# An encoder block on one core: all attention ahead of the MLP, and the MLP as two seven-product passes

## The chip, the core and the metric

The kernel runs on one core of one Trainium2 chip. The core has a matmul engine (TensorE, PE, with its weight loads shown as PEld), VectorE (DVE), ScalarE (ACT), GpSimd (POOL), and SyncE (SP), which here only issues DMAs. The metric is device time in microseconds (us). The kernel before takes 2292.17 us (median of 3 runs, 2291.84 to 2292.46).

## The reference

One layer of a hybrid encoder on 2048 tokens of width 1024, with 16 meta tokens ahead. All arithmetic is to fp32 accuracy.

```python
hn = rms_norm(h, g_mix); proj = hn @ w_in          # 1024 x 1536
q, k, v, u = ...                                   # 4 query heads, 2 key heads of 128; u: 4 groups of 128
q, k = axial_rope(rms_norm(q, g_q)), axial_rope(rms_norm(k, g_k))
attn = softmax(q @ k.T / sqrt(128)) @ v            # all 2064 keys
four = fft2(u).real @ w_fourier                    # per group
h = h + concat(rms_norm(attn), rms_norm(four)) @ w_out
m = rms_norm(h, g_mlp)
h = h + square(relu(m @ w_up)) @ w_down            # 1024 x 4096, 4096 x 1024
return rms_norm(h, g_final)[:, 16:]
```

## The kernel before

**Products.** Most products are split: each fp32 operand becomes hi + lo in a faster format (fp32r), by a cast on ACT and a subtraction on DVE (`split`, L70 and L71, or L73 and L74 with a scale), and `mm3` (L80 to L82) makes three matmuls, hi x hi, hi x lo, lo x hi. A plain fp32 product is one call without splits.

**Attention.** The generator `attention()` works in 16 units: a unit is 256 tokens and one key head with its two query heads, 512 columns. For each of 16 tiles of 128 keys and a last one of 96 rows (`REM`, the meta keys), `scores` makes three matmuls into s, ACT copies s to S, and DVE takes running maxima M of pairs. At the end of a unit `stats` turns M into mb (transposes on PE, a maximum on DVE, transposes, a copy on ACT). `softmax` subtracts mb on DVE, takes exponents on ACT, sums into acc on DVE, and multiplies with v on PE into o. Where a unit is below `NATIVE` (2 here, units 0 and 1), the value product is plain fp32 (L842, o<-S,vn); else the exponent is split (ph on ACT, pl on DVE) and `mm3` is used. While unit u is in `softmax`, unit u+1 is in `scores`, LAG tiles behind. `finish` divides by the row sums and stores o_d. A unit is 20 steps of the generator.

**What stands beside it.** `Att.upto(n)` runs the generator up to step n, and `mix(gen, n, a0, a1)` spreads steps a0 to a1 over the yields of another generator, so attention is laid between other work: the Fourier part (`four`) up to step `FLEAD` = 30, the Fourier half of the out-projection (`out_f`, 32 groups pof of 12 matmuls) up to the end of block 0, then the MLP of blocks 0 and 1 (`head`). A block is 512 tokens (`BLOCKS`). The tile framework orders the instructions of each engine once more when the program is built; the order is fixed from then on.

**The MLP.** The attention half of the out-projection of a block is `out_a` (poa, 96 matmuls), after which h is complete and its norm known. Blocks 0 and 1 go through `transposes`, `up` (pup, 8 groups of 192 matmuls) and `down` (pdn, the same), weights loaded and split once for each block. Blocks 2 and 3 go through one pass of 1024 tokens, in which 2 x 2 blocks of a matrix product are made of seven products instead of eight (`ORDER` = "1265734", with sums and differences of blocks on DVE): `flip_early` and `flip` scale and transpose h (block 2 through m_d in DRAM, by m and mt on ACT), `b_form` makes the seven moving operands BF, `up_weights` loads w_up in pieces R0 and R1 and forms seven stationary operands wuh, wul for each of 8 groups; the up products are ux and uy, stored to s_d in the forms that the down products need; the down products dx and dy are added to h (hs). The final norm and the stores to out follow each tile (`follow`, `store`). The last products of block 1's MLP (`up(1, 7)`, `down(1, 7)`) stand around `out_a(3)`, `flip(3)` and the forming of BF.

PSUM: `bank` takes one of 4 tiles, s and o and the transposes have others, and in the pass `ybank` has 4.

SP issues most DMAs in one order, POOL those of q, k and v.

Of the kernel before, what the change touches and what calls it, by code (L numbers as in the profile page):

```python
# [19 lines left out]
P = 128  # L20
# [20 lines left out]
NATIVE = 2  # L41
# [4 lines left out]
LEAD = 4  # L46
AHEAD = 30
FLEAD = 30
SKIP = 5
T_BUFS = (5, 6)  # L50
F_BUFS = (6, 7)
S_BUFS = 8
A_BUFS = 11
# [82 lines left out]
def encoder_block(ctx: ExitStack, tc: tile.TileContext, x, meta, w_in, w_f,  # L136
# [64 lines left out]
    m_d = dram.tile([P, KT, 512], F32, name="m_d")  # L201
# [530 lines left out]
    ended = []  # L732

    def attention():
# [70 lines left out]
        def softmax(u, i):  # L805
# [4 lines left out]
            if i == NT:  # L810
# [10 lines left out]
                ended[:] = [ins_of(nc.tensor.matmul(s["O"], vt[4][:MR], hi[:MR], start=False, stop=True))]  # L821
# [29 lines left out]
        def finish(u):  # L851
# [16 lines left out]
            if first:  # L868
                sqs[b] = ap2.tile([P, 256], F32, name=f"sq_{b}", tag="sq", bufs=3)
# [28 lines left out]

    HELD = 5
# [9 lines left out]
    def out_f():  # L909
# [103 lines left out]
    hp0 = Lines(tc.alloc_tile_pool(name="hp0", bufs=1, reuse_waits="tile"), small)  # L1013
    op_ = Lines(tc.alloc_tile_pool(name="op", bufs=1, reuse_waits="tile"), small)
    of = out_f()
    mix(itertools.islice(of, 34 - HELD), 34 - HELD, FLEAD, need[0])
    mix(of, HELD, need[0], need[0] + LEAD)
# [3 lines left out]

    hps = hp0, Lines(tc.alloc_tile_pool(name="hp1", bufs=1, reuse_waits="tile"), small)
    atp = Lines(tc.alloc_tile_pool(name="atp", bufs=1, reuse_waits="tile"), small)
    mp = Lines(tc.alloc_tile_pool(name="mp", bufs=1, reuse_waits="tile"), small)
    H, MT = {}, {}
# [4 lines left out]
    SC = {}  # L1030

    def out_a(b, beside=iter(())):
# [15 lines left out]
        sums = [mp.tile([P, 2], F32, name=f"hss_{b}_{t}", tag="hss", bufs=8) for t in range(T)]  # L1048
        A = (atp if b > 1 else ey).tile([P, 2, NQ, 512], R32, name=f"at_{b}", tag="at" if b > 1 else "e0")
# [4 lines left out]
        part = []  # L1054
        for half in range(2):
            c = slice(half * 512, (half + 1) * 512)
            pss = [bank(f"poa_{b}_{half}_{t}") for t in range(T)]
            ops = {}

            def products(t, k):  # L1060
                ts = slice(t * P, (t + 1) * P)
                a, w = ops[k]
                mm3(nc, pss[t], (a[0][:, ts], a[1][:, ts]), w, k == 0, k == NQ - 1)

            for k in range(NQ):
                w = wtile(w_out[k * P:(k + 1) * P, c], f"oa_{b}_{half}_{k}", c_ao(k))
                ops[k] = (A[:, 0, k], A[:, 1, k]), w
                if k < NQ - 2:
                    for t in range(T):
                        products(t, k)  # L1070
                    if half:
                        next(beside, None)
                    yield
            for t in range(T):
                for k in (NQ - 2, NQ - 1):
                    products(t, k)
                if t % 2:
# [12 lines left out]
        for t in range(T):  # L1090
            nc.vector.scalar_tensor_tensor(part[t], sums[t][:, 1:2], 1.0 / D, part[t], op0=ALU.mult, op1=ALU.add)
            if b < 2:
                nc.vector.reciprocal(SC[b][:, t:t + 1], part[t])
                continue
            tag = "rs_m2" if b == 2 else "rs_m"
            ms.append(mp.tile([P, 1], F32, name=f"{tag}_{b}_{t}", tag=tag, bufs=4))
            nc.gpsimd.tensor_tensor(ms[t], part[t], mhalf[:, :1], op=ALU.pow)
            nc.sync.dma_start(h_d[2 * b0 + t], hs[t])
        att.cap = need[b + 1] + AHEAD if b < 3 else 1 << 30

    def transposes(b):

        T = 2 * BLOCKS[b][1]
        mhl = [(ey if b or e == "l" else atp).tile([P, KT, 512], R32, name=f"mT{e}_{b}", tag=tag)
               for e, tag in zip("hl", ("e0" if b else "at", "e1"))]
        MT[b] = [(mhl[0][:, k, :T * P], mhl[1][:, k, :T * P]) for k in range(KT)]
        for kk in range(KT // 2):
            for k in (2 * kk, 2 * kk + 1):
                ps = app.tile([P, 512], F32, name=f"pmt_{b}_{k}", tag="S", bufs=2)
                for t in range(T):  # L1110
                    nc.tensor.transpose(ps[:, t * P:(t + 1) * P], H[b][t][:, k * P:(k + 1) * P], ident)
                split(mhl[0][:, k, :T * P], mhl[1][:, k, :T * P], ps[:, :T * P], c_mlp(k))
            yield

    def flip_early(b):

        hs, ms = H.pop(b), MT[b, "s"]
        for kk in range(KT // 2):
# [3 lines left out]
            for i in range(2):  # L1122
                k = 2 * kk + i
                ps = app.tile([P, 512], F32, name=f"pmt_{b}_{k}", tag="S", bufs=2)
# [4 lines left out]
                nc.sync.dma_start(m_d[:, k], raw)  # L1129
            yield  # L1130

    def up(b, grp):
        N = 256 * BLOCKS[b][1]
        f0 = grp * 512
        pss = [bank(f"pup_{b}_{grp}_{f}") for f in range(4)]
        ws = []
        for k in range(KT):
            w = wtile(w_up[k * P:(k + 1) * P, f0:f0 + 512], f"up_{b}_{grp}_{k}")
            ws.append(w)
            if k < KT - 2:  # L1140
                for f in range(4):
                    fs = slice(f * P, (f + 1) * P)
                    mm3(nc, pss[f][:, :N], (w[0][:, fs], w[1][:, fs]), MT[b][k], k == 0, False)
                yield
        for f in range(4):
            fs = slice(f * P, (f + 1) * P)
            for k in (KT - 2, KT - 1):
                mm3(nc, pss[f][:, :N], (ws[k][0][:, fs], ws[k][1][:, fs]), MT[b][k], False, k == KT - 1)
            if f % 2:
                yield  # L1150
        acts = []
        for f in range(4):
            r = a_tile(f"r_{b}_{grp}_{f}")[:, :N]
            nc.scalar.activation(r, pss[f][:, :N], AF.Relu)  # L1154
            nc.scalar.square(r, r)
            hl = tuple(a_tile(f"a{e}_{b}_{grp}_{f}", R32)[:, :N] for e in "hl")
            split(*hl, r)
            acts.append(hl)
        MT[b, grp] = acts

    def down(b, grp, halves=(0, 1)):
        T = 2 * BLOCKS[b][1]
        f0 = grp * 512
# [4 lines left out]
        if last:  # L1168
            sums = MT[b, "f"]
# [618 lines left out]
```

## Time and profile before

| | |
|---|---|
| median of 3 runs | 2292.17 us (2291.84 to 2292.46) |
| profiled execution: span | 2291.4 us |
| the same execution's granted TensorE clock, mean | 0.999 |
| PE busy | 2278.1 us, 10846 matmuls |
| DVE busy | 1718.7 us |
| ACT busy | 1280.6 us |
| DMA moved | 307.23 MB, mean 134 GB/s |
| first matmul of the seven-product pass | at 1674.2 us |

The profile shows one execution. Its span runs from the first to the last instruction. A row of a group of instructions has line, engine, operation, output and inputs, shapes and count, then busy time in us and the mean of one in ns, then the idle time before them and what ended it. Matmuls are pipelined: one is shown with 390 ns though the next starts some 227 ns later, so the busy time of PE hides short gaps, and its pace (matmuls per us) tells more.

### The profile page before, as it was taken

Reading aid. Unit: us, or ns where it says so; the run is one execution under the profiler, and the core shown is the slowest. Engines: PE = TensorE matmul, PEld = TensorE weight load, DVE = VectorE, ACT = ScalarE, POOL = GpSimd, SP = SyncE. Lnnn points to the kernel's source line nnn. Section 1 sums busy time; section 2 is a strip of 40 time slices with the busy share of each in tenths; the row PEclk is TensorE's granted clock in tenths of the full one; section 3 lists DMA queues with packets and bytes.
Section 4 is the critical chain, followed back from the end, with each engine's and each line's share of the span. In section 5 each row is a group of like instructions: output and inputs, shape, how many; then the busy total and the mean of one; then the engine's idle time right before and its main releaser. Section 6 shows DMA issues by size and latency. Waiting matters only on the chain.

```text
span 2291.4 us, 30005 instructions
## 1 busy us (share of the span) xinstructions
PE 2278.1 (99%) x10846; PEld 1883.0 (82%) x10846; DVE 1718.7 (75%) x2448; ACT 1280.6 (56%) x2303; POOL 184.0 (8%) x235
## 2 busy tenths in 40 slices
PE   9999999999999999999999999999999999999998
PEld 7888988777888888888888888888888888888887
DVE  6435588999986877986887877885875656697796
ACT  6443356566665655665765775664665545543344
POOL 2212120222000000000000100000000000200000
PEclk9999999999999999999999999999999999999999
DMA  6343252543533222333342453224454444865442
GB/s 213 100 119 102 78 169 79 190 137 120 166 117 108 96 87 79 114 114 106 97 157 87 157 175 104 92 82 170 140 177 158 152 152 156 303 193 165 129 138 83
DMA packets 178069, 307.23 MB, mean 134 GB/s; under 512 B 14960, under 2 KB 63728, under 8 KB 177536
## 3 DMA queue, kind: packets, MB, share of 16 engines
q1 hardware_dynamic: 159136, 262.89, 34.9%
q0 software_dynamic: 18640, 42.16, 6.2%
q8 instruction: 85, 1.39, 0.3%
q14 instruction: 64, 0.52, 0.1%
q10 hardware_dynamic: 144, 0.26, 0.0%
HBM read 225.27 MB, written 79.99 MB: 133 GB/s over the span
## 4 chain that ended last, share of the span: by engine, by line
PE 94%; DVE 3%; DMA 1%; ACT 1%; issue 1%; POOL 0%; SPq 0%; POOLq 0%; DVEq 0%; ACTq 0%
PE pdn L80 5%; PE pdn L82 5%; PE pdn L81 5%; PE pup L80 5%; PE pup L82 5%; PE pup L81 5%; PE s L80 3%; PE s L82 3%; PE s L81 3%; PE ux L80 2%; PE ux L81 2%; PE ux L82 2%; PE dx L80 2%; PE dx L82 2%; PE dx L81 2%; PE o L81 2%
## 5 line engine op out<-in xcount | busy, mean ns | idle before, releaser
L80 PE MATMUL pdn<-wh_dn,ah 128*128 128x512 f32 x512 | 201.5, 394 | 0.2 <-ACT r L1154 0.2
L80 PE MATMUL pup<-mTh,wh_up 128*128 128x512 f32 x512 | 201.5, 394 | 0.0
L81 PE MATMUL pup<-mTl,wh_up 128*128 128x512 f32 x512 | 200.7, 392 | 0.0
L82 PE MATMUL pup<-mTh,wl_up 128*128 128x512 f32 x512 | 200.4, 391 | 0.0
L81 PE MATMUL pdn<-wl_dn,ah 128*128 128x512 f32 x512 | 199.9, 390 | 0.0
L82 PE MATMUL pdn<-wh_dn,al 128*128 128x512 f32 x512 | 198.7, 391 | 0.0
L773 ACT COPY S<-s 128x512 f32<-128x512 f32 x256 | 148.4, 584 | 55.6 <-PE s L82 48.5
L70 ACT CAST wh_up<-wr_up 128x512 fp32r<-128x512 f32 x128 | 79.4, 620 | 164.3 <-PE pup L81 76.5
L832 DVE TENSOR_TENSOR S<-S,mb 128x1024 f32<-128x1024 f32 x128 | 154.8, 1218 | 8.4 <-ACT mb L803 8.2
L71 DVE TENSOR_TENSOR pl<-S,ph 128x512 fp32r<-128x512 f32 x196 | 132.3, 696 | 11.0 <-ACT ph L70 10.7
L833 ACT ACTIVATE S<-S 128x1024 f32<-128x1024 f32 x114 | 120.7, 1060 | 34.7 <-DVE S L832 34.1
L70 ACT CAST wh_dn<-wr_dn 128x512 fp32r<-128x512 f32 x128 | 79.1, 620 | 107.9 <-PE pdn L82 52.6
L71 DVE TENSOR_TENSOR wl_up<-wr_up,wh_up 128x512 fp32r<-128x512 f32 x128 | 87.6, 687 | 68.1 <-ACT wh_up L70 63.3
L839 DVE TENSOR_TENSOR acc<-acc,S 128x1024 f32<-128x1024 f32 x110 | 134.1, 1219 | 1.3 <-ACT S L833 1.1
L71 DVE TENSOR_TENSOR wl_dn<-wr_dn,wh_dn 128x512 fp32r<-128x512 f32 x128 | 87.2, 687 | 60.2 <-ACT wh_dn L70 51.8
L70 ACT CAST ph<-S 128x512 fp32r<-128x512 f32 x196 | 118.7, 620 | 15.9 <-PE o L82 12.5
L70 ACT CAST ah<-a 128x1024 fp32r<-128x1024 f32 x56 | 58.5, 1048 | 118.2 <-issue 60.8
L779 DVE TENSOR_TENSOR M<-M,S 128x1024 f32<-128x1024 f32 x96 | 118.0, 1229 | 6.7 <-ACT S L773 6.0
L80 PEld LDWEIGHTS pdn<-wh_dn,ah 128*128 128x128 f32 x512 | 96.1, 188 | 23.5 <-ACT r L1154 3.6
L80 PE MATMUL s<-q,kt 128*128 128x512 f32 (+1 forms) x272 | 113.0, 415 | 0.1
L82 PEld LDWEIGHTS pdn<-wh_dn,al 128*128 128x128 f32 x512 | 96.2, 188 | 19.9
L82 PEld LDWEIGHTS pup<-mTh,wl_up 128*128 128x128 f32 x512 | 96.2, 188 | 19.4
(345 smaller groups left out, 6413.0 us busy)
## 6 DMA issues: line engine op xcount, KB each, us to landing
wr_up<-in_w_up_dram SPq DMA_DIRECT2D x128, 256.0 KB, 2.8
wr_dn<-in_w_down_dram SPq DMA_DIRECT2D x128, 256.0 KB, 2.6
a<-s_d SPq DMA_DIRECT2D x42, 512.0 KB, 3.6
R<-in_w_up_dram SPq DMA_DIRECT2D x16, 1024.0 KB, 5.2
s_d<-s SPq DMA_DIRECT2D x64, 256.0 KB, 2.2
d<-in_w_down_dram SPq DMA_DIRECT2D x26, 512.0 KB, 5.0
s_d<-c SPq DMA_DIRECT2D x48, 256.0 KB, 2.4
x<-in_x_dram SPq DMA_DIRECT2D x16, 512.0 KB, 4.9
```

The lines of the kernel that those rows point to most:

```text
L70: self.high = nc.scalar.copy(hi, src)
L71: self.low = nc.vector.tensor_tensor(lo, src, f32v(hi), op=ALU.subtract)
L80: nc.tensor.matmul(out, a[0], b[0], start=first, stop=False, skip_group_check=chain)
L81: nc.tensor.matmul(out, a[0], b[1], start=False, stop=False, skip_group_check=chain)
L82: nc.tensor.matmul(out, a[1], b[0], start=False, stop=last, skip_group_check=chain)
L773: nc.scalar.copy(S[:, i % 2], ps)
L779: nc.vector.tensor_tensor(M, M, S, op=ALU.max)
L832: nc.vector.tensor_tensor(S, S, mb, op=ALU.subtract)
L833: nc.scalar.activation(p, S, AF.Exp, scale=ISQ)
L839: nc.vector.tensor_tensor(acc, acc, p, op=ALU.add)
```

## The change

- All 16 units make their value products in plain fp32 (`NATIVE` = 16), so v is loaded unsplit and p is not split.
- `up`, `down`, `transposes`, `flip_early`, `final` and `head` are gone. `out_a` keeps all of w_out's attention half in SBUF as splits (WO), goes tile by tile, and every block is turned by `flip` into m_d.
- Attention is laid beside the Fourier part up to step 84 (`FLEAD`), beside `out_f` up to step 210 (`OLEAD`), then 31 steps beside `out_a` and `flip` of block 0 and as many beside those of block 1; what is left is issued at the first yield of `out_a(2)`. `out_a(3)` and `flip(3)` come after attention.
- Then `up_pass` and `down_pass` run twice, for blocks 0 and 1 (pass 0) and 2 and 3 (pass 1). Beside pass 0's up products, `forms_ahead` makes the moving operands of pass 1 and stores them to f_d; pass 1 loads them.

```diff
-NATIVE = 2
+NATIVE = 16
-LEAD = 4
-AHEAD = 30
-FLEAD = 30
+FLEAD = 84
+OLEAD = 210
+STEPS_A = 31
-A_BUFS = 11
+A_BUFS = 6
...
-    m_d = dram.tile([P, KT, 512], F32, name="m_d")
+    m_d = [dram.tile([P, KT, 512], F32, name=f"m_d{b}") for b in range(4)]
+    f_d = {n: dram.tile([P, 2, 4, 512], F32, name=f"f_d{n}") for n in ORDER}
...
-    mix(itertools.islice(of, 34 - HELD), 34 - HELD, FLEAD, need[0])
-    mix(of, HELD, need[0], need[0] + LEAD)
+    mix(out_f(), 34, FLEAD, OLEAD)
...
+        MS[b] = ms = []
+        for t in range(T):
+            ts = slice(t * P, (t + 1) * P)
+            sums = mp.tile([P, 2], F32, name=f"hss_{b}_{t}", tag="hss", bufs=8)
+            for half in range(2):
+                c = slice(half * 512, (half + 1) * 512)
+                ps = bank(f"poa_{b}_{half}_{t}")
+                for k in range(NQ):
+                    mm3(nc, ps, (A[:, 0, k, ts], A[:, 1, k, ts]), WO[k, half], k == 0, k == NQ - 1)
+                nc.vector.scalar_tensor_tensor(hs[t][:, c], ps, ra[:, t:t + 1], hs[t][:, c], op0=ALU.mult, op1=ALU.add)
+                nc.scalar.activation(a_tile(f"hj_{b}_{t}_{half}"), hs[t][:, c], AF.Square,
+                                     accum_out=sums[:, half:half + 1])
+                yield
...
+    for b in range(3):
+        a0 = OLEAD + b * STEPS_A
+        mix(itertools.chain(out_a(b), flip(b)), 12 if b < 2 else 9, a0, a0 + STEPS_A if b < 2 else 1 << 20)
...
+    def forms_ahead(lf):
+
+        for k, i in itertools.product(range(4), range(2)):
+            r, c = {}, slice(i * 256, i * 256 + 256)
+            for n, b, kk in (("11", 2, k), ("21", 2, k + 4), ("12", 3, k), ("22", 3, k + 4)):
+                r[n] = lf.tile([P, 256], F32, name=f"lr{n}_{k}_{i}", tag="lr" + n)
+                nc.sync.dma_start(r[n], m_d[b][:, kk, c])
+
+            def keep(name, src):
+                t = lf.tile([P, 2, 256], R32, name=f"lf{name}_{k}_{i}", tag="lf", bufs=2)
+                split(t[:, 0], t[:, 1], src)
+                nc.sync.dma_start(f_d[name][:, :, k, c], f32v(t))
...
+    for r, b, k in ((b11, 0, 0), (b21, 0, 4), (b12, 1, 0), (b22, 1, 4)):
+        nc.sync.dma_start(r, m_d[b][:, k:k + 4])
+    b_form(ey, "1", b11, tag="e0")
+    b_form(bf2, "2", b21)
+    drain(out_a(3))
+    minus(b11, b12, b11)
+    drain(flip(3))
...
+    up_pass(0, sp, pc, UW, ready, first_down(0, sp, FIRST), hs, forms_ahead(lf))
...
+    down_pass(0, sp, FIRST, hs)
+    sp = right("sp1")
+    UW = up_weights(1, sp)
+    bfb = left("bfb")
+    for name in ORDER:
+        t = bf_tile(ey, name, tag="e0") if name == "7" else bf_tile(bfb, name)
+        nc.sync.dma_start(f32v(t), f_d[name])
+        if name in "126":
+            ready.append(next(UW))
+    pc = right("pc1")
+    hs, FIRST = [], []
+    up_pass(1, sp, pc, UW, ready, first_down(1, sp, FIRST), hs, iter(()))
+    pc.release()
+    bfb.release()
+    down_pass(1, sp, FIRST, hs)
```

Where the instructions stand now. PE in attention, while unit 13 is in `softmax` and unit 14 in `scores` (o_13 is a value product, s_14_10 the scores of key tile 10), before:

```order
L82 MATMUL s_14_10_13651<-q_14_13206,kt_6_0_2_13212 128x512
L80 MATMUL pup_1_3_0_13523<-mTh_1_11165,wh_up_1_3_4_13659 128x512
L81 MATMUL pup_1_3_0_13523<-mTl_1_11166,wh_up_1_3_4_13659 128x512
L82 MATMUL pup_1_3_0_13523<-mTh_1_11165,wl_up_1_3_4_13660 128x512
L80 MATMUL pup_1_3_1_13524<-mTh_1_11165,wh_up_1_3_4_13659 128x512
L81 MATMUL pup_1_3_1_13524<-mTl_1_11166,wh_up_1_3_4_13659 128x512
L82 MATMUL pup_1_3_1_13524<-mTh_1_11165,wl_up_1_3_4_13660 128x512
```

and in the changed kernel:

```order
L84 MATMUL s_14_10_8453<-q_14_8255,kt_6_0_2_8261 128x512
L85 MATMUL s_14_10_8453<-q_14_8255,kt_6_0_2_8261 128x512
L845 MATMUL o_13_8252<-S_13_12_8105,vn_4_1_3_6780 128x512 x2
L83 MATMUL s_14_11_8462<-q_14_8255,kt_6_0_2_8261 128x512
L84 MATMUL s_14_11_8462<-q_14_8255,kt_6_0_2_8261 128x512
L85 MATMUL s_14_11_8462<-q_14_8255,kt_6_0_2_8261 128x512
L83 MATMUL s_14_12_8470<-q_14_8255,kt_6_0_3_8263 128x512
```

Before, twelve up products stand between two steps of attention; now nothing does.

SP at the end of attention (ohl_15 is the last unit's output, at_3 the pieces of block 3's attention output, b11 and b21 the moving operands' sources, R0 and R1 pieces of w_up), before:

```order
L864 DMA o_d3_3471<-ohl_15_15297 128x2x256 x2
L979 DMA wr_dn_1_6_1_2_15465<-in_w_down_dram 128x512
L1052 DMA at_3_15528<-o_d3_3471 128x512 x2
L979 DMA wr_dn_1_6_1_3_15483<-in_w_down_dram 128x512
L1052 DMA at_3_15528<-o_d3_3471 128x512 x2
L979 DMA wr_oa_3_0_0_15541<-in_w_out_dram 128x512
L1312 DMA b11_15756<-m_d_130 128x2048
```

and in the changed kernel:

```order
L1105 DMA R1_0_0_9069<-in_w_up_dram 128x4x512
L1074 DMA m_d2_132<-mt_2_6_9043 128x512
L1074 DMA m_d2_132<-mt_2_7_9051 128x512
L1495 DMA b11_9087<-m_d0_130 128x2048
L1495 DMA b21_9088<-m_d0_130 128x2048
L1495 DMA b12_9089<-m_d1_131 128x2048
L1495 DMA b22_9090<-m_d1_131 128x2048
L1041 DMA at_3_9124<-o_d3_3481 128x512 x3
```

Before, the pieces of at_3 are loaded right behind the stores of ohl_15; now the last three of them stand behind the stores of block 2's turned rows and four loads of 1 MB.

SP between the two passes, which has no counterpart before (hs0_1 is the second half of pass 0's rows, bf1 to bf6 the moving operands that pass 1 loads); before, the loads of R0 and R1 for the only pass stand among the weights of block 1:

```order
L979 DMA wr_oa_3_0_3_15583<-in_w_out_dram 128x512
L1270 DMA R0_0_15991<-in_w_up_dram 128x4x512
L979 DMA wr_oa_3_1_0_15637<-in_w_out_dram 128x512
L1270 DMA R1_0_15993<-in_w_up_dram 128x4x512
L979 DMA wr_oa_3_1_1_15655<-in_w_out_dram 128x512
```

and in the changed kernel:

```order
L1403 DMA out_dram<-hs0_1_12165 128x512 x6
L1534 DMA bf1_14314<-f_d1_134 128x4096
L1105 DMA R0_1_0_14316<-in_w_up_dram 128x4x512
L1105 DMA R1_1_0_14318<-in_w_up_dram 128x4x512
L1534 DMA bf2_14326<-f_d2_135 128x4096
L1534 DMA bf6_14332<-f_d6_136 128x4096
```

The first loads of pass 1 stand behind all stores of pass 0.

More of the change, by code (lines that the diff above doesn't have):

```diff
@@ L1099, in out_a @@
[L1099 to L1113, printed above, removed]
@@ L1128, in flip_early @@
                 nc.scalar.activation(raw, ps, AF.Copy, scale=c_mlp(k))
-                nc.sync.dma_start(m_d[:, k], raw)
+                nc.sync.dma_start(m_d[b][:, k], raw)
             yield
[L1132 to L1159, printed above, removed]
@@ L1576, in encoder_block @@
-    part = [small.tile([P, 1], F32, name=f"epm_{t}", tag=("rs_m2", "ms_m")[t // 4], bufs=4) for t in range(8)]
-    def first(t, half):
-        square(t, half)
-        nc.vector.tensor_scalar(part[t], sums[t][:, half:half + 1], 1.0 / D, EPS, op0=ALU.mult, op1=ALU.add)
-        v = hs[t][:, halves[half]]
-        nc.vector.tensor_tensor(v, v, gfin[half], op=ALU.mult)
-    def norm_part(t, v):
-        return ins_of(nc.vector.scalar_tensor_tensor(part[t], v, 1.0 / D, part[t], op0=ALU.mult, op1=ALU.add))
@@ L1588, in norm @@
-    def norm(t, half, share=None):
-        end = norm_part(t, sums[t][:, half:half + 1] if share is None else share)
-        rs = small.tile([P, 1], F32, name=f"ers_{t}", tag="rs_m", bufs=4)
-        nc.gpsimd.tensor_tensor(rs, part[t], mhalf[:, :1], op=ALU.pow)
-        done.append((t, half, rs))
-        return end
-    def store(t, half, rs):
-        v, z = hs[t][:, halves[half]], hs[t][:, halves[1 - half]]
-        nc.vector.scalar_tensor_tensor(v, v, rs, gfin[half], op0=ALU.mult, op1=ALU.mult)
-        nc.scalar.activation(z, z, AF.Copy, scale=rs)
-        for h, w in ((half, v), (1 - half, z)):
-            eng = nc.scalar if t == 7 and w is z else nc.sync
-            eng.dma_start(out[(8 + t) * P:(9 + t) * P, halves[h]], w)
@@ new lines, in encoder_block @@
+    sp = right("sp0")
+    UW = up_weights(0, sp)
+    ready = [next(UW), next(UW)]
+    bf2 = right("bf2")
+    rs_ = right("rs")
+    b11, b21, b12, b22 = (rs_.tile([P, 4, 512], F32, name=f"b{n}", tag=f"b{n}") for n in ("11", "21", "12", "22"))
+    for r, b, k in ((b11, 0, 0), (b21, 0, 4), (b12, 1, 0), (b22, 1, 4)):
[5 more added lines that the diff above has]
+    drain(flip(3))
@@ new lines, in encoder_block @@
+    mp.release()
+    for pool in hps[::-1]:
+        pool.release()
+    wp.release()
+    bfa = left("bfa")
+    ready += [next(UW)]
+    t5 = bf_tile(bfa, "5")
+    t6 = bf_tile(bfa, "6")
+    for c in (slice(0, 2), slice(2, 4)):
+        split(t5[:, 0, c], t5[:, 1, c], b11[:, c])
+    minus(b11, b22, b11)
+    for c in (slice(0, 2), slice(2, 4)):
+        split(t6[:, 0, c], t6[:, 1, c], b11[:, c])
+    minus(b12, b22, b12)
+    b_form(bfa, "7", b12)
+    b_form(bfa, "3", b22)
+    minus(b21, b21, b11)
```

796 lines of the change are left out of this document (334 added, 462 removed).

## The prediction

> **What bounds the kernel now.** I read the page's busy times, then the busy time of each engine in four stretches, cut at the first copy of mb (the running maxima, once for each of 16 attention units), after four units, at the first matmul of the seven-product pass and at its last.
>
> ```profile
> span 2291.4 us, 30005 instructions
> PE 2278.1 (99%) x10846; PEld 1883.0 (82%) x10846; DVE 1718.7 (75%) x2448; ACT 1280.6 (56%) x2303; POOL 184.0 (8%) x235
> PE 94%; DVE 3%; DMA 1%; ACT 1%; issue 1%; POOL 0%; SPq 0%; POOLq 0%; DVEq 0%; ACTq 0%
> ...
> core 0: us, PE busy (x) PEld busy (x) DVE busy (x) ACT busy (x) POOL busy (x), PEclk, DMA share, GB/s
> 344.90:452.60 107.70, 107.05 (x576) 83.39 (x575) 99.69 (x138) 65.66 (x115) 19.50 (x24) 1.00 0.43 129
> 452.60:570.50 117.90, 116.83 (x526) 92.27 (x525) 113.59 (x159) 74.37 (x145) 26.66 (x35) 1.00 0.40 133
> 570.50:1674.20 1103.70, 1102.97 (x5010) 903.56 (x5009) 881.60 (x1226) 688.11 (x1175) 45.74 (x55) 1.00 0.37 118
> 1674.20:2284.80 610.60, 609.97 (x2701) 504.98 (x2699) 428.02 (x504) 289.46 (x392) 22.36 (x37) 1.00 0.49 166
> ...
> L803 ACT COPY mb<-pd_m x16: 567/587/589, 344.9 to 1507.0; 128x512 f32<-128x512 f32 x16
> ```
>
> PE bounds every stretch, and MLP matmuls are why: they fill PE while attention keeps DVE busy. In the second stretch (units 2 and 3, beside out-projections alone) DVE too is busy for 113.59 of 117.9 us, 96%. From 570 us on it is at 80%. The pure pass has 2701 matmuls in 610.6 us: 0.226 us each.
>
> **What is removed and added on PE.**
>
> ```profile
> L80 PE MATMUL pup<-mTh,wh_up 128*128 128x512 f32 x512 | 201.5, 394 | 0.0
> L80 PE MATMUL pdn<-wh_dn,ah 128*128 128x512 f32 x512 | 201.5, 394 | 0.2 <-ACT r L1154 0.2
> ...
> L842 PE MATMUL o<-S,vn 128*128 128x512 f32 x64 | 30.4, 596 | 0.0
> ...
> 405.22 0.40 PE L81 MATMUL s<-q,kt 128*128 128x512 f32 x1
> 405.45 0.40 PE L82 MATMUL s<-q,kt 128*128 128x512 f32 x1
> ...
> 405.85 1.72 PE o L842 x4
> ```
>
> The direct MLP has three matmuls of each of these two kinds, 6 x 512 = 3072. By seven products it is 2688: 384 x 0.226 = 87 us less. A plain fp32 value product is two instructions in the trace (64 for 2 units of 16 products); four take 1.72 us, so a product takes 0.86 us. The split form is three matmuls, 0.68 to 0.69 us (0.23 apart in the timeline here). 14 units x 16 x 0.175 = 39 us more. If PE stayed full, the change would gain about 48 us. So the question is whether it stays full.
>
> **Attention without the MLP beside it.** Value products in fp32 take no splits, which frees DVE and ACT, but what remains is this:
>
> ```profile
> L832 DVE TENSOR_TENSOR S<-S,mb 128x1024 f32<-128x1024 f32 x128 | 154.8, 1218 | 8.4 <-ACT mb L803 8.2
> L839 DVE TENSOR_TENSOR acc<-acc,S 128x1024 f32<-128x1024 f32 x110 | 134.1, 1219 | 1.3 <-ACT S L833 1.1
> L779 DVE TENSOR_TENSOR M<-M,S 128x1024 f32<-128x1024 f32 x96 | 118.0, 1229 | 6.7 <-ACT S L773 6.0
> L781 DVE TENSOR_TENSOR M<-M 128x512 f32<-128x512 f32 x16 | 11.5, 720 | 0.3
> L817 DVE TENSOR_TENSOR ph<-S,ph 32x512 fp32r<-32x512 f32 x16 | 12.0, 750 | 0.9 <-PE s L82 0.4
> L957 DVE SCALAR_TENSOR_TENSOR xo<-pof,rs_f,xo 128x512 f32<-128x512 f32 x32 | 23.7, 741 | 1.8 <-PE pof L82 1.5
> ...
> L773 ACT COPY S<-s 128x512 f32<-128x512 f32 x256 | 148.4, 584 | 55.6 <-PE s L82 48.5 <-DVE pl L71 1.6 <-DVE acc L837 1.3
> L833 ACT ACTIVATE S<-S 128x1024 f32<-128x1024 f32 x114 | 120.7, 1060 | 34.7 <-DVE S L832 34.1
> ```
>
> For a pair of key tiles DVE does one maximum, one subtraction and one sum: 3 x 1.22 = 3.66 us. PE does six score matmuls and two value products: 6 x 0.226 + 1.72 = 3.08 us. ACT does 2 x 0.584 + 1.06 = 2.23 us. So alone, attention is DVE's: 22 such steps (26.9 us) and some 11 of half size at about 0.7 make 34.9 us a unit, PE 27.
>
> I counted each engine's instructions between mb copies in the changed order and priced them by the means of their forms. Units 0 to 5, beside the Fourier part and the first out-projections: DVE 254, PE 225. Units 6 to 12, beside the rest of them and two attention projections: DVE 283, PE 297. Units 13 and 14, with little beside them: DVE 73, PE 68. How such a sum turns into time is read from the trace: the same count for before's units 2 and 3 gives DVE 120.4 and they took 117.9; its native units 0 and 1 give 105.0 and took 107.7. So DVE's sum is the time where it is the larger (recorded durations overlap a little, and waits take that back). I take 254; 305 for the middle, PE's sum and 3% because DVE is near; 76 at the end. That is 635 us from mb of unit 0 to mb of unit 15. Bounds: PE's own 590 plus 3%, 608; and DVE's 610 with 8% of waits, 660. I take the middle since DVE's rows lie nearest.
>
> **The end of attention.** Before, up and down products of block 1 cover the last projection and the turn of block 3. Now nothing does.
>
> ```profile
> L1121 ACT ACTIVATE m<-h,rs_m 128x256 f32<-128x256 f32 x16 | 7.3, 507 | 0.7 <-POOL rs_m L1097 0.7
> L1128 ACT ACTIVATE mt<-pmt,cols 128x512 f32<-128x512 f32 x8 | 5.1, 684 | 0.0
> ...
> R<-in_w_up_dram SPq DMA_DIRECT2D x16, 1024.0 KB, 5.2
> a<-s_d SPq DMA_DIRECT2D x42, 512.0 KB, 3.6
> o_d<-ohl SPq DMA_DIRECT2D x32, 256.0 KB, 2.5
> at<-o_d SPq DMA_DIRECT2D x32, 256.0 KB, 4.3
> ```
>
> Counted from unit 15's mb: DVE needs 15 large steps and unit 14's finish, 22 us, then some 5 to the last row sums and h. The turn of block 2 is ACT's, 16 x 0.507 + 8 x 0.684 = 13.6 us, and ends at 42. SP then issues the 1 MB loads b11, b21, b12, b22, and behind them the last three pieces of at_3, without which no poa_3 product can end. From 512 KB to 1 MB adds 1.6 us, so a MB is 3.2 us; the 5.5 MB in the queue are 17.6 and about 2 of latency: they land at 61. PE meanwhile has 19 matmuls of product 2 (4.3 us). The other 88 of poa_3 end at 81. The turn of block 3 then waits for the last sum, square and power (3 us), and its ACT work ends at 95; product 1 follows it. PE's work in these 95 us is 54, so 41 are lost. Bounds: 80 (loads land as they are issued close together) and 108.
>
> **The two passes.** Pass 0 has 2664 matmuls left, 605 us, and 3 us for its operands, whose splits and differences (some 20 us of DVE) start late. The operands of pass 1 that it forms beside (56 splits of 256 columns and 32 differences) are some 37 us of DVE and 24 of ACT over 305 us; DVE has 30% free there and ACT half, so they cost nothing; without that cover they would cost 37. Pass 1 is the old pass, from its first matmul to the end of the span: 2291.4 - 1674.2 = 617.2.
>
> ```profile
> L80 PE MATMUL ux<-bf,wuh x192: 389/389/389, 1674.2 to 1978.3; 128*128 128x512 f32 x192
> L82 PE MATMUL dy<-bh,al x196: 279/389/389, 1991.0 to 2284.5; 128*128 128x512 f32 x192, 128*128 128x256 f32 x4
> ...
> L1636 DVE TENSOR_TENSOR hs<-hs,dx 128x512 f32<-128x512 f32 x64 | 43.2, 683 | 26.3 <-PE dx L82 26.0
> L1574 ACT ACTIVATE ej<-hs 128x512 f32<-128x512 f32 x15 | 9.5, 632 | 22.5 <-DVE hs L1636 22.5
> L1574 ACT ACTIVATION_READ_ACCUMULATOR ej<-hs 128x1 f32 x15 | 2.8, 186 | 0.0
> L1591 POOL TENSOR_TENSOR ers<-epm,mhalf 128x1 f32<-128x1 f32 x8 | 4.4, 549 | 266.7 <-DVE epm L1586 266.7
> L1598 ACT ACTIVATE hs<-hs,ers 128x512 f32<-128x512 f32 x8 | 5.7, 712 | 1.7 <-POOL ers L1591 1.7
> L70 ACT CAST wuh<-R 128x1024 fp32r<-128x1024 f32 x32 | 33.7, 1054 | 37.5 <-PE ux L81 24.5 <-PE uy L81 11.4 <-DMA R<-in_w_up_dram 1.4
> ...
> 2288.00:2291.40 3.40, 0.00 (x0) 0.00 (x0) 0.00 (x0) 0.00 (x0) 0.00 (x0) 0.52 0.41 154
> ```
>
> Between the passes is a new gap. SP is in order, and pass 0's last stores stand ahead of bf1, R0, R1, bf2. The last store waits for add, square with its read-out, power and scale: 0.68 + 0.63 + 0.19 + 0.55 + 0.72 and hops, 3.6 us after the last matmul. Then bf1 (2 MB, 8.4 by the slope above; between 5.2, the row of 1 MB, and 10.4), R0 behind it (3.2) and its cast (1.05): 16.4 us without PE. bf2 and bf6, 2 MB each for products of 5.4 us, come 2.4 us late. Together 19, between 12 and 26.
>
> **Sum.** 344.9 to the first mb (PE's order up to there has the same work, 319 us of matmuls in both) + 635 + 95 + 605 + 3 + 19 + 617.2 = 2319 as a span. The runs' median is 0.8 us above the profiled span; 2319 stands.
>
> **The clock.** With PE idle, the granted clock is 0.52 over the last 3.4 us (row above): it fell some 3 us after the last matmul. [...] From rows: if a gap's clock stays low for 3 us after it, those 3 us do half their work, 1.5 us for each of three gaps and a few shorter ones, 2325.
>
> **Rivals.**
> - The clock falls in the gaps: 2325, chance 0.15. For it: the row of 0.52. Against: single transposes inside the turns may hold it up.
> - Attention waits more (maximum, transposes, mb, subtraction, exponent in a row at every unit's end, with nothing beside): 660 instead of 635, 2344, chance 0.14. For it: units 0 and 1 above took more than their sum.
> - Faster: attention runs at PE's pace, with DVE's steps overlapping fully: 600 instead of 635, 2284, chance 0.09. It decides once that stretch is under 607. For it: groups' busy times are a few per cent under count x mean; against it: 96% DVE in units 2 and 3.
> - The two load queues cost nothing: poa_3 starts at 37 instead of 60 (18 saved, since product 2 then no longer fills), and bf1 and R0 are ahead (13): 2288, chance 0.07, no change.
>
> **How the numbers follow.** My forecast has 0.55, 2319, its own range 2305 to 2335. A measurement can tell 0.2% (4.6 us): faster 0.09, same 0.07, slower 0.84. The range from 2288 to 2347 leaves out about a tenth on each side.
>
> **What would show it.** DVE over 92% busy and PE at some 88% of matmul pace between the first mb and unit 15's; a stretch of about 40 us with less than half PE's work, then ux; a gap of 15 to 20 us between the last dx of one pass and the first ux of the next; o<-S,vn at 0.86 a product. I am wrong if DVE is under 88% there with PE full, or if bf1 lands before the last matmul.

## The result, and the profile after

The changed kernel takes 2366.06 us (median of 4 runs, 2363.92 to 2366.94); the kernel before, on the same chip, 2292.32 (2291.84 to 2292.61). The ratio is 1.032, 95% interval 1.0306 to 1.0335. It is slower by 74 us, where 27 were forecast. The profiled execution took 2365.9 us, its span is 2364.0.

The head of the page, and of its 40 slices the rows of PE and of the granted clock:

```profile
span 2364.0 us, 28292 instructions
PE 2265.3 (96%) x10238; PEld 1785.3 (76%) x10238; DVE 1706.1 (72%) x2266; ACT 1197.8 (51%) x2061; POOL 218.5 (9%) x269
...
PE   9999999999999999967999999999969999999998
...
PEclk9999999999999999978999999999989999999999
```

PE has 608 matmuls less than before and yet ends later: it is busy for 96% instead of 99%, and in the slices of the two stage changes the clock falls. The busy time by stages (the same columns as the stretches of before), cut at the first and the last copy of mb, at pass 0's first ux, at its last dx and at pass 1's first ux:

```profile
core 0: us, PE busy (x) PEld busy (x) DVE busy (x) ACT busy (x) POOL busy (x), PEclk, DMA share, GB/s
0.00:346.50 346.50, 340.99 (x2032) 297.99 (x2033) 194.57 (x415) 162.13 (x475) 68.90 (x83) 1.00 0.43 129
346.50:997.50 651.00, 625.49 (x2567) 426.86 (x2567) 572.09 (x704) 389.82 (x661) 104.42 (x111) 0.99 0.36 115
997.50:1094.00 96.50, 72.05 (x273) 49.14 (x271) 55.90 (x77) 51.54 (x96) 5.47 (x8) 0.81 0.47 167
1094.00:1720.40 626.40, 612.94 (x2672) 504.52 (x2670) 456.41 (x574) 305.18 (x443) 19.30 (x33) 0.98 0.56 189
1720.40:1740.00 19.60, 0.17 (x1) 0.00 (x0) 2.28 (x5) 3.10 (x5) 0.55 (x1) 0.64 1.00 384
1740.00:2364.00 624.00, 613.68 (x2700) 506.75 (x2700) 424.80 (x492) 286.02 (x383) 19.84 (x34) 0.99 0.51 178
```

Beside the forecast's terms this gives:

| stage | forecast | measured | over |
|---|---|---|---|
| to the first mb | 344.9 | 346.5 | 1.6 |
| attention, first to last mb | 635 | 651.0 | 16.0 |
| last mb to the first ux | 95 | 96.5 | 1.5 |
| rest of pass 0 | 608 | 626.4 | 18.4 |
| between the passes | 19 | 19.6 | 0.6 |
| pass 1 | 617.2 | 624.0 | 6.8 |

So the excess over the forecast, 45 us of span, lies in attention and in the two MLP passes. The end of attention and the gap between the passes cost what was forecast.

Within attention, the stretches of units 0 to 5, 6 to 12, and 13 and 14, for which the prediction had 254, 305 and 76:

```profile
346.50:600.20 253.70, 241.70 (x1053) 166.77 (x1053) 236.35 (x295) 155.15 (x253) 38.58 (x43) 0.99 0.31 92
600.20:922.00 321.80, 311.55 (x1237) 213.16 (x1236) 268.19 (x331) 186.01 (x327) 59.51 (x59) 0.99 0.42 136
922.00:997.50 75.50, 72.24 (x282) 46.93 (x281) 67.55 (x78) 48.66 (x81) 6.33 (x9) 1.00 0.32 106
```

All of attention's excess lies in the middle one.

### The profile page after: what moved, and what is told of

Its sections match the earlier page's. It is cut to its first block, busy times and chain, and to the rows that moved or that the text cites. A ratio compares the mean times of both kernels' runs of the same rounds, so it can differ in the third digit from the quotient of the medians.

```text
span 2364.0 us, 28292 instructions
## 1 busy us (share of the span) xinstructions
PE 2265.3 (96%) x10238; PEld 1785.3 (76%) x10238; DVE 1706.1 (72%) x2266; ACT 1197.8 (51%) x2061; POOL 218.5 (9%) x269
## 4 chain that ended last, share of the span: by engine, by line
PE 61%; DVE 7%; DMA 7%; ACT 3%; issue 3%; POOL 0%; SPq 0%; DVEq 0%; POOLq 0%; ACTq 0%
PE o L845 6%; PE dx L84 5%; PE dx L83 5%; PE dx L85 5%; PE dy L84 4%; PE dy L85 4%; PE dy L83 4%; PE ux L83 3%; PE ux L85 3%; PE ux L84 3%; PE uy L84 3%; PE uy L85 3%; PE uy L83 3%; PE s L83 2%; DMA q<-q_d 2%
## 5 line engine op out<-in xcount | busy, mean ns | idle before, releaser
L845 PE MATMUL o<-S,vn 128*128 128x512 f32 x512 | 246.0, 601 | 4.6 <-ACT S L836 4.5
L83 PE MATMUL ux<-bf,wuh 128*128 128x512 f32 x512 | 202.7, 396 | 28.3 <-ACT wuh L73 19.4
L83 PE MATMUL dx<-bh,ah 128*128 128x512 f32 x512 | 200.1, 391 | 2.8 <-ACT bh L73 1.5
L84 PE MATMUL dx<-bl,ah 128*128 128x512 f32 x512 | 199.9, 390 | 2.3 <-DVE bl L74 2.3
L84 PE MATMUL ux<-bf,wuh 128*128 128x512 f32 x512 | 201.8, 394 | 0.0
L85 PE MATMUL ux<-bf,wul 128*128 128x512 f32 x512 | 201.6, 394 | 0.0
L85 PE MATMUL dx<-bh,al 128*128 128x512 f32 x512 | 199.6, 390 | 0.0
L83 PE MATMUL uy<-bf,wuh 128*128 128x512 f32 x384 | 150.7, 393 | 10.5 <-ACT bf L73 9.8
L83 PE MATMUL dy<-bh,ah 128*128 128x512 f32 (+1 forms) x388 | 150.6, 388 | 1.4 <-ACT ah L73 1.4
L84 PE MATMUL uy<-bf,wuh 128*128 128x512 f32 x384 | 150.8, 393 | 0.9 <-DVE bf L74 0.9
L85 PE MATMUL dy<-bh,al 128*128 128x512 f32 (+1 forms) x388 | 150.6, 388 | 0.9 <-DVE al L74 0.9
L85 PE MATMUL uy<-bf,wul 128*128 128x512 f32 x384 | 150.6, 392 | 0.0
L83 PEld LDWEIGHTS ux<-bf,wuh 128*128 128x128 f32 x512 | 97.8, 191 | 50.1 <-ACT wuh L73 19.9
L74 DVE TENSOR_TENSOR wul<-R,wuh 128x1024 fp32r<-128x1024 f32 x64 | 78.3, 1223 | 79.3 <-ACT wuh L73 77.4
```

The costliest lines, as they stand in the source:

```text
L74: self.low = nc.vector.tensor_tensor(lo, src, f32v(hi), op=ALU.subtract)
L83: nc.tensor.matmul(out, a[0], b[0], start=first, stop=False, skip_group_check=chain)
L84: nc.tensor.matmul(out, a[0], b[1], start=False, stop=False, skip_group_check=chain)
L85: nc.tensor.matmul(out, a[1], b[0], start=False, stop=last, skip_group_check=chain)
L845: nc.tensor.matmul(s["O"], v[:, 2 * j % 4 + e], p[:, e], start=i + e == 1, stop=False)
```

## The experiments

### What paces attention

The waits of PE, and of DVE, in the changed kernel's attention (engine, line waited with, releaser; us in total, times, longest):

```profile
PE s L83 <- DMA q<-q_d: 14.1, 11, 2.1
...
DVE S L835 <- ACT mb L806: 21.8, 11, 3.7
DVE M L782 <- ACT S L776: 20.2, 18, 3.0
```

PE is busy for 625.5 of 651 us there (96%), DVE for 572.1 (87.9%): just under the 88% that the prediction named as a sign of being wrong. But PE is not full. Its recorded times hide short gaps; with each matmul taken at the time from its start to the next one's in the same trace (0.227 us for a split one, 0.43 for one of a value product, 0.11 for a transpose, 0.12 for the Fourier part's), its work there is an estimated 598 us, 92%. What PE waits for most is q. There is one q buffer: the load of the next unit's q is issued when the last score of the unit before is done, and the next unit's scores find it still in flight. Three runs: take the wait away, take DVE work away, take PE work away.

**A second q buffer**

```diff
-q = (ap if u else ap2).tile(..., tag="q" if u else "acc", bufs=1)
+q = (ap if u else ap2).tile(..., tag="q" if u else "acc", bufs=2 if u else 1)
...
```

> A second buffer for q, so that a unit's q load no longer waits for the last score product of the unit before (room made by one buffer instead of two for the small tiles ph and pl). Theory A (PE paces attention, and what PE waits for at a unit's head is the q load: 15.8 us in 12 waits in the trace of the changed kernel): the waits vanish, attention from the first mb to the last falls from 651 to 636-640 us, the time to 2350-2354 us. Theory B (DVE paces attention, PE's wait for q is cover for DVE's work): attention stays within 4 us of 651, the time at 2362-2368 us.

2345.62 us (2344.45 to 2346.34), 20.4 less; ratio to before 1.0232 (1.0217 to 1.0247). Attention in its trace:

```profile
345.20:977.60 632.40, 623.14 (x2574) 424.46 (x2573) 571.41 (x706) 390.61 (x662) 105.48 (x110) 1.00 0.36 118
```

The stretch is 632.4 us instead of 651, PE is busy for 98.5% of it (by the same estimate, 599 us of work, 95%), and no wait for q is left. Theory A holds, with a little more than it promised. Units 0 to 5 take 244.2 us, units 6 to 12 312.1. The 33 us that PE's work leaves are short waits that no run takes apart.

**Fewer sums on DVE**

```diff
...
-if j == 1 and s["native"]:
+if 1 < j < 7:
+    pass
+elif j == 1 and s["native"]:
```

> Five of the seven additions of exponentials in each unit are left out (80 additions of 1024 columns, 1.14 us each back to back: 91 us of DVE's 572 in attention; a constant is added to the sums that remain). Theory A (PE paces attention): attention falls by no more than 15 us, from waits at unit heads, the time to 2351-2364 us. Theory B (DVE paces): attention falls to PE's own work, 608 us and the q waits of 13, so by 30 us or more, the time to 2325-2336 us.

2358.73 us (2356.03 to 2366.02). Between the first mb and the last:

```profile
345.00:988.40 643.40, 618.81 (x2563) 423.89 (x2562) 491.84 (x630) 388.57 (x660) 90.83 (x110) 1.00 0.36 116
...
DVE M L782 <- ACT S L776: 82.0, 53, 5.0
```

With 80 us less to do (491.8 busy), DVE gave back 7.6 us of time; most of the rest became waiting for scores (82 us instead of 20). Theory A holds: DVE does not pace attention.

**Fewer score matmuls on PE**

```diff
-mm3(nc, ps[:rows], (kt[:, 0, k0:k0 + rows], kt[:, 1, k0:k0 + rows]), s["q"], True, True)
+nc.tensor.matmul(ps[:rows], kt[:, 0, k0:k0 + rows], s["q"][0], start=True, stop=False)
+nc.tensor.matmul(ps[:rows], kt[:, 0, k0:k0 + rows], s["q"][1], start=False, stop=True)
```

> The third matmul of each score product is left out (the low part of the keys): 16 x 17 x 0.227 = 62 us of PE less, 58 of it between the first mb and the last. Theory A (PE paces attention): attention falls by 35 us or more, until DVE's 610 paces it, the time to 2325-2331 us. Theory B (DVE paces): attention falls by less than 15 us, the time to 2351-2364 us.

2344.44 us (2340.57 to 2349.18).

```profile
345.50:975.40 629.90, 582.74 (x2314) 383.29 (x2313) 568.75 (x703) 387.97 (x662) 133.38 (x110) 0.98 0.37 120
...
PE s L765 <- DMA q<-q_d: 21.3, 12, 4.1
```

Attention is 21 us shorter, between the two theories' marks (35 or more, under 15). Of 58 us of PE work taken out, a third came back as time; then PE (92%), DVE (90%) and longer waits for q (21.3) hold it together. So PE's work counts for more than DVE's, but the time is neither engine's sum: waits between them, for q above all, stand beside it. How much of what is left is DVE's limit and how much is q's, this run does not show.

### The price of the fp32 value products

**The kernel before, with them alone**

```diff
-NATIVE = 2
+NATIVE = 16
```

> The kernel before with one part of the change alone: the value products of all 16 units in plain fp32 (14 units more than before). Theory A (where PE is full, an fp32 product costs its 0.175 us more than a split one and nothing else): 224 x 0.175 = 39 us more, 2331 us (2325-2337). Theory C (an fp32 product among others also delays the product after it, by up to 0.05 us): 2338-2345 us. Theory D (the splits that fall away on DVE and ACT give PE something back): under 2322 us.

2332.44 us (2331.70 to 2333.14), ratio 1.0175 (1.016 to 1.019). The page's PE row, and the group of the products:

```profile
PE 2318.8 (99%) x10622; PEld 1844.2 (79%) x10622; DVE 1588.4 (68%) x2224; ACT 1166.1 (50%) x2079; POOL 187.9 (8%) x235
...
L842 PE MATMUL o<-S,vn 128*128 128x512 f32 x512 | 243.1, 594 | 0.1
```

PE stays full, and 224 products cost 40.1 us, 0.179 each against 0.175 forecast. That DVE has 130 us less to do (1718.7 to 1588.4) gives nothing. This half of the change alone makes the kernel slower. No run has the changed kernel with split value products, so what they cost there, where PE is not full, is not shown.

### The end of attention

SP's issues in the changed kernel (start, duration, engine and line, what):

```profile
1025.93 1.10 SPq L867 DMA_DIRECT2D o_d<-ohl  x2
...
1028.17 0.37 SPq L1041 DMA_DIRECT2D at<-o_d  x1
...
1039.94 0.89 SPq L1074 DMA_DIRECT2D m_d<-mt  x2
1040.88 2.19 SPq L1495 DMA_DIRECT2D b<-m_d  x4
1043.12 2.62 SPq L1041 DMA_DIRECT2D at<-o_d  x3
...
1051.83 1.22 PE L83 MATMUL uy<-bf,wuh 128*128 128x512 f32 x2 [9.79 <-ACT bf L73]
```

The output of the last unit is stored from 1025.9 us on, but the last three loads of at_3 stand in SP's queue behind the turn of block 2 and the four MB of b, as forecast. PE waits 9.8 us, for b.

**at_3 first**

```diff
+a3 = out_a(3)
+next(a3)
 for r, b, k in ((b11, 0, 0), (b21, 0, 4), ...):
...
-nc.sync.dma_start(f32v(A[:, e, k]), o_d[b][:, e, k])
+(nc.gpsimd if b == 3 else nc.sync).dma_start(f32v(A[:, e, k]), o_d[b][:, e, k])
...
-drain(out_a(3))
+drain(a3)
```

> The loads of at_3 (the last block's attention output) go out on POOL's queue and ahead of the four 1 MB loads of b, whose forms are made behind them. Theory A (SP's order holds the last projection: at_3's last three pieces were issued at 1043 us, 17 us after their data was stored): poa_3 runs from about 1032 us, before product 2 instead of behind it; the wait of 9.8 us for the cast of b is gone or lies in the turn of block 3; the turn of block 3 ends 15 to 25 us sooner, the time is 2341-2352 us. Theory B (the turn of block 2 on ACT and the forms of b set when product 1 begins, whatever the projection does): under 5 us, 2361-2367 us.

2351.09 us (2342.07 to 2352.31), 15 less. In the trace the last pieces go out at once, and the wait is gone:

```profile
1030.72 2.18 POOL L1041 DMA_DIRECT2D at<-o_d  x4 [3.91 <-issue]
...
PE pmt L1071 <- ACT m L1066: 5.4, 3, 2.3
```

From the last mb (999.6) to the first ux (1078.9) it is 79.3 us instead of 96.5. Theory A holds: SP's order was the path. The run moves two things at once, the loads to another queue and the last projection ahead of product 2 on PE; the two were not tried apart.

**Both together**

> The second q buffer and the early loads of at_3 together. Theory A (two separate waits on one path): the savings of the single runs add, 20 + 15 us off 2366: 2327-2334 us. Theory B (what attention saves at its end runs into the same chain of the turn of block 2 and the loads): less than 28 us in all, 2338 us or more.

2329.51 us (2328.37 to 2330.95), ratio 1.0161 (1.0146 to 1.0177): 36.6 us less, and 20.4 + 15.0 = 35.4. The two waits are separate and add. This is as fast as any variant of the changed kernel was, and still 37 us slower than before.

**Projections later**, on top of both:

```diff
-OLEAD = 210
-STEPS_A = 31
+OLEAD = 225
+STEPS_A = 38
```

> The second q buffer, the early at_3, and attention taken ahead of the out-projections (225 of its steps by the end of the Fourier out-projection instead of 210, 38 steps beside an attention projection instead of 31), so that more of the projection of block 2 is left for the time after attention. Theory A (PE-paced attention gets shorter by the work that leaves it, and that work fills the 30 us in which PE lacks work afterwards): 2316-2326 us. Theory B (attention is then paced by DVE's 572 us and its unit heads, and the turns of blocks 2 and 3 follow each other on ACT): no gain or a loss against the same without this shift, 2328-2340 us.

2330.26 us (2328.04 to 2331.03), the same. Attention is 626.4 us instead of 632.3, but the way from its end to the first ux 85.9 instead of 78.8. What left the one stretch came back in the other: theory B, without its loss.

### The start of pass 0

Product 2's last matmul ends at 1107.5 us, and product 6 waits. PE's wait, and ACT's and DVE's work ahead of its end:

```profile
PE ux L83 <- ACT p L1218: 8.8, 1, 8.8
...
1099.97 7.75 ACT L73 CAST bf<-b 128x1024 fp32r<-128x1024 f32 x8
...
1113.66 2.18 ACT L73 CAST bf<-b 128x1024 fp32r<-128x1024 f32 x2 [3.45 <-DVE b L1143]
1115.75 0.58 ACT L1218 COPY p<-ux 128x512 f32<-128x512 f32 x1
...
1112.41 2.35 DVE L1143 TENSOR_TENSOR b<-b,b 128x1024 f32<-128x1024 f32 x2
```

Product 6 is added to product 1 in the same PSUM tile, so product 1 must be copied out (p) first. The copy is half a microsecond, but on ACT it stands behind ten casts of the operands 5, 6, 7, 3 and 4, and the last two of these wait for DVE's differences. Operand 4 is needed four products after product 6.

**Fewer forms**

```diff
-b_form(bfa, "7", b12)
-b_form(bfa, "3", b22)
+BF["7"], BF["3"], BF["4"] = BF["5"], BF["6"], BF["5"]
...
-b_form(bfa, "4", b21)
```

> In pass 0 the operands 7, 3 and 4 of the tokens are not formed (others stand in for them): six casts on ACT, six subtractions for their low parts and four differences on DVE less. Theory A (product 6 waits 8.8 us for the copy of product 1, which stands on ACT behind the cast of operand 4, and that behind DVE's differences): the wait falls under 3 us, the clock does not fall to 0.5 there, product 6 begins 6 to 9 us after the last turn instead of 15, the time is 2354-2359 us. Theory B (operands 5 and 6 alone keep ACT and DVE as long): the wait stays over 6 us, the time 2362-2367 us.

2350.82 us (2347.61 to 2355.32), 15.2 less, three beyond theory A's mark. Theory A holds: product 6 does not wait for p, PE is full from 1095 to 1125 us, and the clock is 0.96 there:

```profile
1095.00:1125.00 30.00, 30.00 (x137) 24.70 (x136) 15.58 (x26) 21.91 (x41) 0.00 (x0) 0.96 0.72 241
```

In this trace pass 0 takes 609.9 us from its first ux to the end of its last product, against 626.6 in the changed kernel's.

### The gap between the passes, and the clock

SP around the end of pass 0, and the cast that pass 1 waits for:

```profile
1717.86 0.33 SPq L1534 DMA_DIRECT2D bf<-f_d  x1
1719.26 5.49 SPq L1403 DMA_DIRECT2D out_dram<-hs  x6
1724.80 1.00 SPq L1534 DMA_DIRECT2D bf<-f_d  x1
1726.26 2.18 SPq L1105 DMA_DIRECT2D R<-in_w_up_dram  x2
...
1738.90 1.04 ACT L73 CAST wuh<-R 128x1024 fp32r<-128x1024 f32 x1 [15.22 <-DMA R<-in_w_up_dram]
```

The load at 1717.86 is bf7, into the one tile that is free early; bf1 follows the last store, and R0 follows bf1, as in the prediction.

**bf1 early**

```diff
-t = bf_tile(ey, name, tag="e0") if name == "7" else bf_tile(bfb, name)
+t = bf_tile(ey, name, tag="e0") if name == "1" else bf_tile(bfb, name)
```

> Between the passes, the operand that is loaded early into the tile that frees first is bf1, needed first, instead of bf7; R0 and R1 then follow the last stores with no 2 MB load ahead of them. Theory A (the gap of 19.4 us is the load queue: bf1's 2 MB and then R0): R0 lands some 5 us after its issue at 1725 us, its cast is done at 1731 us, the gap is 9 to 12 us, the time 2356-2360 us. Theory B (R0's 12.6 us come from all the loads in flight sharing the bandwidth, whatever their order): the gap stays over 16 us, the time 2362-2367 us.

2365.56 us (2362.58 to 2368.40), no change. PE's longest waits in its trace, at the start of pass 1's up and of its down products:

```profile
PE ux L83 <- DMA R<-in_w_up_dram: 14.3, 1, 14.3
...
PE dy L83 <- ACT ah L73: 6.1, 1, 6.1
```

The gap is 14.3 us, between the theories: R0 took 8.9 us from issue to its cast, not 5, with the DMA engines full (share 1.05, 405 GB/s). And it is given back: POOL issued the first loads of the down pass 282.0 us after pass 1's first ux (2018.2), behind a uy product, instead of 276.0 (2016.0), behind a ux product, and the down pass's first dy waits 6.1 us instead of 1.4. That the loads come later because the tile of bfb that frees first now holds bf2 and not bf1 is read from the code, not tried.

**R on ACT's queue as well**

```diff
-nc.sync.dma_start(r, w_up[...])
+(nc.scalar if p and not g else nc.sync).dma_start(r, w_up[...])
```

> As the run with bf1 early, and R0 and R1 of pass 1 go out on ACT's queue, so that they stand behind no store. Theory A: R0 is issued when the last matmul of pass 0 has freed its place (1720.7 us) and lands at 1726, the gap is 6 to 8 us, the time 2352-2357 us, the fall of the clock no longer counts or by 1 us only. Theory B: as with bf1 early alone, since R0 shares the bandwidth with the last stores and bf2: within 2 us of that run.

2365.65 us (2364.75 to 2367.96). R0 is issued at 1719.6 us, and is cast at 1733.1, 13.5 us later; the gap is 12.8 us, the later wait 6.5. Theory B has the time. R0 is cast 1.9 us sooner than with bf1 early alone (1735.1 there), but R1 2.3 us later (1740.0 against 1737.7). So it looks as if the loads and the last stores share one bandwidth, and an earlier place in a queue only moves who waits.

**A busy gap**

```diff
+pw = bank("pwarm")
+for _ in range(75):
+    nc.tensor.matmul(pw[:, :P], ident, ident, start=True, stop=True)
 sp = right("sp1")
```

> 75 products of 128 columns, whose result is not used, on PE in the gap between the passes (16 of its 19.4 us). Theory A (the granted clock of 0.5 after a gap costs time): the clock stays at 1.0, the first 24 matmuls of pass 1 take 5.6 us instead of 8.8, the span falls by 3 us to about 2361 us. Theory B (the first matmuls wait for the second half of their operand, not for the clock): they take over 8 us still, the span within 1.5 us of 2364.

One run, 2360.40 us. Its span is 5.5 us shorter, but 3.5 of these were there by the last mb. The stretches from the unused products on, with the granted clock in the third column from the end:

```profile
1716.50:1731.90 15.40, 15.40 (x139) 15.30 (x138) 1.05 (x3) 1.63 (x4) 0.55 (x1) 1.00 1.00 393
1731.90:1736.70 4.80, 1.56 (x6) 0.95 (x6) 1.23 (x1) 1.04 (x1) 0.00 (x0) 1.00 1.09 425
1736.70:1740.10 3.40, 3.40 (x9) 2.62 (x9) 3.20 (x3) 1.20 (x2) 0.00 (x0) 0.52 1.01 429
```

The products ran out 2.7 us before pass 1 could begin, and the clock fell after all, at 1736.7 us, when PE was at work again. The first 24 matmuls took 8.1 us. So this run decides neither theory; the next has more of these products, and no rest.

**A busy gap without a rest**, on top of q and at_3:

> The second q buffer, the early at_3, and 96 unused products of 128 columns in the gap between the passes (19.7 us at the 0.205 us that they took in the run with 75 of them, so that PE runs out less than 1 us before the operands are there or up to 2 us after). Theory A (a gap of some 3 us already brings the clock down to 0.5; no gap, no fall): the clock stays at 1.0, the first 24 matmuls of pass 1 take under 6.5 us instead of 8.1 to 9.0, and from the last dx of pass 0 to the end it is 1 to 3.5 us less than without them. Theory B (the fall comes from the start of the loads or from the first matmuls themselves): those 24 take over 7.5 us.

2330.31 us (2326.80 to 2331.46), against 2329.51 without. The gap and the first 24 matmuls after it, without the unused products (first two rows, the run with both changes) and with them:

```profile
1684.70:1704.60 19.90, 0.14 (x1) 0.00 (x0) 2.26 (x4) 3.02 (x5) 0.55 (x1) 0.56 0.99 376
1704.60:1713.40 8.80, 8.63 (x24) 6.42 (x25) 7.12 (x6) 2.66 (x4) 0.00 (x0) 0.64 1.02 432
```

```profile
1685.40:1706.40 21.00, 21.00 (x190) 21.00 (x190) 2.90 (x5) 3.10 (x5) 0.55 (x1) 1.00 1.01 386
1706.40:1712.10 5.70, 5.70 (x28) 4.58 (x26) 5.40 (x6) 2.70 (x3) 0.00 (x0) 1.00 1.01 430
```

The clock stays at 1.00 and the 24 matmuls take 5.7 us instead of 8.8: it is the gap that brings the clock down. Theory A is right on the clock, but not on the time: from the end of pass 0 to the end of the span it is 644.2 us, against 644.3. Of the 3.1 us, 1.3 went to the gap, which is longer than without the unused products (21.2 us against 19.9), and 1.7 were lost again in pass 1. There the clock falls at the first down products, from 2025.1 to 2031.9 us, with PE busy for 6.0 of these 6.8, so an estimated 3.0 lost; without the unused products it does not fall there. PE's listed waits there are not the cause: they add up to 2.9 us, against 3.8 without. So a fall that was avoided in one place came in another, and what one costs on this path is less than these runs can tell.

## Why the prediction was right or wrong

**Right: the sign, and why.** The saving of 384 matmuls is there and is outweighed, since PE waits in attention and runs out of work at the stage changes. The fp32 products cost 0.179 us each where PE is full (forecast 0.175).

**Right: the end of attention and the gap.** 96.5 us (95) and 19.6 (19), with the causes named: the 1 MB loads ahead of at_3 (17 us of that stretch, by the run with at_3 first, which also moved the projection on PE), and bf1 and R0 behind the last stores. at_3's last three pieces were issued between 1043.1 and 1045.7 us and took 12.6 to land, so they were there by 1058, 61 us after the last mb, which was the forecast. One detail is not as forecast: the turn of block 3 ended at 100.5 (its last copy by 1098.0 us), not at 95, and product 1 began among its transposes rather than behind it. That the stretch came out so near is in part luck.

**Wrong: attention's waits.** The step that failed is the term for units 6 to 12, 305 us: PE's sum of 297 and 3% for its waits. They took 321.8, and this is the whole excess of 16. The sum itself was sound (by the start-to-start times above PE's work there is an estimated 299 us, and in all of attention 598, against the prediction's 590). What was too small is the 3%: it has no wait for q. The second buffer takes 9.7 us off this stretch and 18.6 off the whole of attention; the other 7 us of the stretch's excess stay open.

The 254 for units 0 to 5 came true (253.7) by luck, since the rule behind it, that DVE's sum is the time where it is the larger, does not hold. DVE's sum was 610 for all of attention by the mean durations of its forms, but DVE is busy for 572, because recorded durations overlap: back to back, an operation shown with 1.22 us starts 1.135 us after the one ahead. With 80 us less to do DVE gave back 7.6. And with the second q buffer units 0 to 5 took 244.2, less than DVE's sum. So the two engines stood in the wrong order, and neither one's sum is the time. The rows on q could have told: in before, POOL's load of q waits for the last score 14 times, as it does after (11 times, second row), but there PE has no wait for q on its list, since other products fill the flight, and only after does PE wait for it (third row):

```profile
  POOL q L744: 357.1, 14
```

```profile
  POOL q L747: 53.4, 11
  PE s L83: 15.8, 12
```

The prediction named the cover that other steps lose, not this one's.

**Wrong: the start of pass 0.** "3 us for its operands" is the term that failed most; it was 18.4 too small: 8.8 are the wait for p behind ten casts, which the prediction had as "some 20 us of DVE" and not as a place in ACT's queue, with what stands behind it. The rest is the clock (two falls there, and one at the first down products, an estimated 8.6 us by the rows below) and 3.8 us of waits for the first down operands (2.3 and 1.5). The run with fewer forms took 15.2 us off by the first cause and the falls that go with it (from 1095 to 1125 us, where the second lies, the clock is 0.96 there instead of 0.79). The waits at the start of the down products were not tried apart. In pass 1 they are 3.6 us, and the fall of the clock at its start 3.0: its 6.8 over the forecast.

**Wrong in size: the clock.** It was a rival at 0.15, with 1.5 us a gap, 2325. The 3 us of low clock after a gap were an estimate: between the passes the clock stays low for 6.2 us from the first ux on. It happened at every stage change. Four of the falls, at the start of pass 0 (two), at its first down products, and between the passes:

```profile
1087.30:1097.50 10.20, 7.12 (x27) 5.10 (x26) 0.85 (x2) 7.32 (x17) 0.00 (x0) 0.51 0.51 177
1111.20:1121.40 10.20, 5.02 (x12) 3.96 (x13) 9.97 (x12) 4.59 (x7) 0.00 (x0) 0.50 0.32 103
1411.50:1418.40 6.90, 5.04 (x12) 3.68 (x13) 6.64 (x10) 6.09 (x9) 2.43 (x5) 0.51 0.87 321
1725.60:1746.00 20.40, 5.96 (x13) 4.29 (x14) 5.64 (x5) 2.16 (x3) 0.00 (x0) 0.50 1.04 411
```

The first lies in the turn of block 3, whose transposes did not hold the clock up. In the last, matmuls start 0.43 us apart at the 0.50, and 0.23 apart behind it. PE is busy for 23.1 us in these four, so an estimated half of that, 11.6 us, is lost: 2.5 to 3.6 a fall, about twice the forecast. Over the whole span, added up in steps of 1 us, the clock is at 0.5 for 92 us, with PE busy in 51 of them; 17 of these lie at the end of attention, where loads and turns are the path.

**The rivals.** "Attention waits more" (2344, at 660) came nearest, for attention at 651; it alone would not have made 2366. The time lies outside the range because three terms were too small at once: attention by the wait for q, pass 0 by its start, and pass 1 by a fall of the clock and later operands. The trace of before has none of these waits, and the rivals were priced one at a time.

## What to carry to other kernels

When covering work is taken away from a stage, list each load that is issued by the release of a single buffer: its flight was free under the cover and becomes a wait once a unit, and a second buffer takes it back (18.6 us of attention here). A short copy that frees a PSUM tile should not stand in an engine's order behind operands that are needed much later: here the copy took 0.58 us, stood behind ten casts, and PE waited 8.8 us. Fewer matmuls gain nothing where the new order costs more in waits than they save: here each stage change cost a wait, and then a stretch at half the clock (5.0 to 7.1 us of PE's work in each of the four rows above). When an engine's work is summed, the time that its neighbours' waits add has to be a term of its own.

## What the runs showed of the hardware

In the trace of the changed kernel the granted clock is at 0.5 in eight stretches ahead of the end, of 3.4 to 30.7 us, and PE does work in each of them. Between the passes it fell 5.1 us after the end of pass 0's last matmul and came back 6.2 us after the start of pass 1's first. In the run with a busy gap a wait of 2.7 us was followed by 3.4 us at 0.52; in the run without a rest the clock stayed at 1.00 there. What decides when it falls and when it comes back, these runs do not show.

Between the passes the loads seem to be held by one bandwidth: with the DMA share at 0.99 to 1.09 the core moved 376 to 432 GB/s, and a 1 MB load of w_up took 8.9 to 13.5 us from its issue to its cast, on SP's queue (8.9 with bf1 early, 12.6 in the changed kernel) as on ACT's (13.5), against the 5.2 to landing of the prediction's row.
